# Sliding windows cut from an image batch: from 16-row bands of half the channels to 8-row bands of all channels

## The chip, the cores and the metric

The kernel runs on one core of a Trainium2 chip. The metric is the device time in microseconds (us) of one execution; before the change the median of three runs is 193.44 us (193.0 to 193.72). Profiles are of one execution each. In a profile ACT is ScalarE, DVE is VectorE, POOL is GpSimd and SP is SyncE; DMA engines are the 16 units that move data between the chip's memory (HBM) and the on-chip memory SBUF, which has 128 partitions.

## What is computed

The input `x` has 16 images of 64 channels of 64 by 64 float32 numbers. The output holds every window of 8 by 8 at a stride of 4, so 15 by 15 windows of each image, each with all channels:

```python
result = np.zeros((batch, n_h, n_w, c, window_size, window_size), dtype=np.float32)
for i in range(n_h):
    for j in range(n_w):
        h_start = i * stride
        w_start = j * stride
        result[:, i, j] = x[:, :, h_start:h_start + window_size, w_start:w_start + window_size].copy()
```

Nothing is calculated; numbers are only moved. 16.8 MB go in and 59.0 MB come out, because neighbouring windows overlap. In the output, one window of one image is a contiguous piece of 16 KB: 64 channels times 64 numbers of 4 bytes.

## The kernel before

**Layout.** A partition holds one image, one half of the channels (`ch`, 32 channels) and one of four bands of 16 image rows (`hq`), in the order image, half, band: partition = 8*image + 4*half + band. The tile `L` keeps the whole input in SBUF, 128 KB per partition.

**Loads (lines 49 to 54).** Four chunks of 8 channels, and in each chunk one DMA per band, 16 DMAs of 1 MB. Even bands are issued on SP's queue and odd ones on ACT's. A DMA goes to every fourth partition, and its contiguous rows are 16 image rows of one channel, 4 KB. Four DMAs can be in flight on each of the two queues; a later one waits for an earlier one of its own queue.

**Windows (`window`, lines 97 to 133).** A window position (j, s) says which column j of 15, and which of the four starting rows s inside a band; it makes 128 windows at once, one on each partition. The numbers of all 128 are gathered into a contiguous tile `G`: for s = 0, 1, 2 by one ScalarE copy (line 111). For s = 3, called last, the window runs over the lower edge of the band: VectorE copies the upper half (line 113) and fetches the lower half from the next partition with a stream shuffle (line 114). In the lowest band there is no such window, so a last position has 96 windows and 32 unused partitions.

**Stores (lines 124 to 133).** One indirect DMA of GpSimd (a scatter) writes the 128 rows of `G` to output rows whose numbers stand in a small index tile: `idx`, or `idx_last`, in which the unused partitions have a number that is out of bounds, so that their rows are dropped. A row is half a window, 8 KB. The tiles' framework tracks the scatters by eight semaphores in turn, so a scatter waits for the one eight places earlier. Different stores are declared independent of each other (`free`, line 88).

**Order.** There are 60 window positions, j outside and s inside. The first 12 (`EARLY`, line 135) are made twice, for the first and the second half of the partition's channels: the first halves need only the first two load chunks, so stores can begin when half of the input is there. Such half scatters have 4 KB rows and index tiles of their own (`idx_h`, `idx_hlast`). Second halves and whole windows then alternate (lines 140 to 145). `G` is a ring of nine buffers of 8 KB per partition, counted in 18 half units (line 93); a window is gathered once the scatter that used its buffer has landed. The last two positions (`TAIL`, line 85) go out by seven plain DMAs of SP (line 118), and take buffers that come free a little earlier (`BACK`, line 148).

The functions that the change touches, with the profile's line numbers:

Of the kernel before, what the change touches and what calls it, by code (L numbers as in the profile page):

```python
# [1 line left out]

# [4 lines left out]


@with_exitstack  # L10
def kernel(
    ctx: ExitStack,
    tc: tile.TileContext,
    x: bass.AP,
    window_size: int,
    stride: int,
    out: bass.AP,
):
    nc = tc.nc
    P = nc.NUM_PARTITIONS  # L20

    B, C, H, W = x.shape
    Bo, NH, NW, Co, WSo, WSo2 = out.shape
    WS = int(window_size)
    ST = int(stride)
    assert Bo == B and Co == C and WSo == WS and WSo2 == WS

    f32 = mybir.dt.float32
    i32 = mybir.dt.int32
    ALU = mybir.AluOpType  # L30
    HQ = 4
    CH = P // (B * HQ)
    CL = C // CH
    RB = H // HQ
    NSLOT = RB // ST
    NWIN = NH * NW
    CFREE = CL * WS * WS
    assert HQ == 4 and CH == 2 and WS == 2 * ST

    lpool = ctx.enter_context(tc.tile_pool(name="lpool", bufs=1))  # L40
    ipool = ctx.enter_context(tc.tile_pool(name="ipool", bufs=1))
    gpool = ctx.enter_context(tc.tile_pool(name="gpool", bufs=1))


    L = lpool.tile([P, CL, RB, W], f32)
    x_v = x.rearrange("b (ch cl) (hq r) w -> hq (b ch) cl (r w)", ch=CH, hq=HQ)
    NCH = 4
    cw = CL // NCH
    for k in range(NCH):
        for q in range(HQ):  # L50
            (nc.sync, nc.scalar)[q % 2].dma_start(
                out=L[q::HQ, k * cw : (k + 1) * cw, :, :],
                in_=x_v[q, :, k * cw : (k + 1) * cw, :],
            )


    def itile(name):
        return ipool.tile([P, 1], i32, name=name)

    pi, tb, tq, tc_, idx, idx_last = (itile(n) for n in ("pi", "tb", "tq", "tc", "idx", "idx_last"))  # L60
    nc.gpsimd.iota(pi[:, :], pattern=[[0, 1]], base=0, channel_multiplier=1)  # L61
    nc.vector.tensor_scalar(out=tb[:, :], in0=pi[:, :], scalar1=3, scalar2=None, op0=ALU.logical_shift_right)  # L62
    nc.vector.tensor_scalar(out=tc_[:, :], in0=pi[:, :], scalar1=2, scalar2=1, op0=ALU.logical_shift_right, op1=ALU.bitwise_and)  # L63
    nc.vector.tensor_scalar(out=tq[:, :], in0=pi[:, :], scalar1=HQ - 1, scalar2=None, op0=ALU.bitwise_and)  # L64
    nc.vector.tensor_scalar(out=tb[:, :], in0=tb[:, :], scalar1=float(NWIN * CH), scalar2=None, op0=ALU.mult)  # L65
    nc.vector.tensor_tensor(out=tb[:, :], in0=tb[:, :], in1=tc_[:, :], op=ALU.add)  # L66
    nc.vector.tensor_scalar(out=tc_[:, :], in0=tq[:, :], scalar1=float(NSLOT * NW * CH), scalar2=None, op0=ALU.mult)  # L67
    nc.vector.tensor_tensor(out=idx[:, :], in0=tb[:, :], in1=tc_[:, :], op=ALU.add)  # L68

    nc.vector.tensor_scalar(out=tq[:, :], in0=tq[:, :], scalar1=float(HQ - 1), scalar2=float(2 * B * NWIN * CH), op0=ALU.is_equal, op1=ALU.mult)  # L70
    nc.vector.tensor_tensor(out=idx_last[:, :], in0=idx[:, :], in1=tq[:, :], op=ALU.add)  # L71


    HCL = CL // 2
    idx_h, idx_hlast = itile("idx_h"), itile("idx_hlast")
    for d, e in ((idx_h, idx), (idx_hlast, idx_last)):
        nc.vector.tensor_scalar(out=d[:, :], in0=e[:, :], scalar1=2.0, scalar2=None, op0=ALU.mult)  # L77
    o_v = out.rearrange("b i j (ch cl) r w -> (b i j ch) (cl r w)", ch=CH)
    o_h = out.rearrange("b i j (ch cl) r w -> (b i j ch) (cl r w)", ch=2 * CH)
    nxt = [min(p + 1, 31) for p in range(32)]  # L80

    order = [(j, s) for j in range(NW) for s in range(NSLOT)]


    TAIL, BACK = 2, 3
    o_q = out.rearrange("b i j (ch cl) r w -> i j b ch (cl r w)", ch=CH)

    def free(st):
        tc.declare_no_dep(st.ins, group="stores", reason="each store writes rows of its own")
        tc.add_to_no_dep_group("stores", st.ins)  # L90


    UNITS = 18
    G = [gpool.tile([P, 2 * HCL, WS, WS], f32, name=f"G{n}") for n in range(UNITS // 2)]
    at = 0

    def window(j, s, half):
        nonlocal at
        cols = slice(j * ST, j * ST + WS)
        last = s == NSLOT - 1  # L100
        if half is None:
            n, c0 = 2, 0
            at += at % 2
        else:
            n, c0 = 1, half * HCL
        u = at % UNITS
        at += n
        cs = slice(c0, c0 + n * HCL)
        g = G[u // 2][:, u % 2 * HCL : (u % 2 + n) * HCL, :, :]
        if not last:  # L110
            nc.scalar.copy(out=g, in_=L[:, cs, s * ST : s * ST + WS, cols])  # L111
        else:
            nc.vector.tensor_copy(out=g[:, :, 0:ST, :], in_=L[:, cs, s * ST : RB, cols])  # L113
            nc.vector.stream_shuffle(out=g[:, :, ST:WS, :], in_=L[:, cs, 0:ST, cols], mask=nxt)  # L114
        if (j, s) in order[-TAIL:]:
            g_q = g.rearrange("(m q) c r w -> q m (c r w)", q=HQ)
            for q in range(HQ - 1 if last else HQ):
                free(nc.sync.dma_start(out=o_q[q * NSLOT + s, j], in_=g_q[q]))
            return
        if half is None:  # L120
            o, ix = o_v, (idx_last if last else idx)
        else:
            o, ix = o_h, (idx_hlast if last else idx_h)
        st = nc.gpsimd.indirect_dma_start(  # L124
            out=o,
            out_offset=bass.IndirectOffsetOnAxis(ap=ix[:, 0:1], axis=0),
            in_=g.rearrange("p c r w -> p (c r w)"),
            in_offset=None,
            element_offset=(s * NW + j) * CH * CFREE + (half or 0) * HCL * WS * WS,
            bounds_check=B * NWIN * CH * (1 if half is None else 2) - 1,  # L130
            oob_is_err=False,
        )
        free(st)

    EARLY = 12
    for j, s in order[:EARLY]:
        window(j, s, 0)
    late = list(order[:EARLY])
    rest = list(order[EARLY:])
    while late:  # L140
        for w in late[:2]:
            window(*w, 1)
        for w in rest[:2]:
            window(*w, None)
        late, rest = late[2:], rest[2:]
    for w in rest[:-TAIL]:
        window(*w, None)
    at -= 2 * BACK
    for w in rest[-TAIL:]:
        window(*w, None)  # L150


# [1 line left out]
_INS = ['x', 'window_size', 'stride']  # L154
_OUTS = [((16, 15, 15, 64, 8, 8), 'float32')]

_NUMBERS = {'window_size': 8, 'stride': 4}


# [26 lines left out]
```

## Time and profile before

| What | Value |
|---|---|
| Median of three runs | 193.44 us |
| The profiled execution's own time | 193.19 us |
| Its span, first to last instruction | 191.4 us |
| ACT busy | 86.2 us (45%) |
| POOL busy | 68.0 us (36%) |
| DVE busy | 30.4 us (16%) |
| HBM read and written | 16.78 and 62.65 MB, 415 GB/s over the span |
| DMA packets | 14772, 75.80 MB |

How to read it. The page gives each engine's busy time, and then cuts the span into 40 equal slices of 4.8 us: a digit is the busy share in tenths, and for the DMA engines a second line gives GB/s. Next come the DMA queues: q1 and q10 hold the DMAs of SP and ACT, q0 the scatters of GpSimd; for each the packets, the megabytes, and the time that its packets took as a share of 16 engines' span. A packet here is one row of a transfer, or one of the 4-byte packets that report a DMA's end on an engine, or the 4-byte stand-in of a dropped row. Then follow the chain of work that ended last, the costliest groups of instructions by line, and the DMA issues with the median time from issue to landing. Other views list who waited for whom, the instructions in order of time, and the same figures for a chosen window of time.

Two durations by form that are used below: the ScalarE copy of 128x2048 takes 1896 ns and that of 128x1024 takes 1040 ns; the stream shuffle of 128x1024 takes 1280 ns and that of 128x512 takes 712 ns. A scatter instruction occupies GpSimd for 963 ns.

### The profile page before, as it was taken

What the parts mean: (1) busy time and instruction counts of PE and PEld (TensorE: products, weight loads), DVE (VectorE), ACT (ScalarE), POOL (GpSimd) and SP (SyncE); (2) the same over time, 40 slices, a digit from 0 to 9 for tenths busy, and PEclk for the clock granted to TensorE, in tenths of its full rate; (3) what the DMA queues carried; (4) which work ended last, traced back from release to release, by engine and by line L of the source; (5) the groups of instructions that cost most, each with busy time, mean ns of one, the idle gap of its engine ahead of it and who ended that gap; (6) DMA issues with size and microseconds to landing.
All of it is one profiled execution on the core that took longest, in us unless ns stands there. A gap on an engine that the chain in (4) does not pass through costs nothing.

```text
span 191.4 us, 479 instructions
## 1 busy us (share of the span) xinstructions
DVE 30.4 (16%) x65; ACT 86.2 (45%) x55; POOL 68.0 (36%) x75
## 2 busy tenths in 40 slices
DVE  2000050000232302301221031203030303000030
ACT  0000059400699876364566556565647473300300
POOL 0000028723367666464464343434444444400000
DMA  5999999999999999999999999999999999999785
GB/s 180 419 413 410 410 409 413 416 423 420 417 423 429 423 418 425 407 406 414 410 413 404 414 416 413 404 409 409 411 407 409 411 409 406 416 411 416 325 265 187
DMA packets 14772, 75.80 MB, mean 396 GB/s; under 512 B 2032, under 2 KB 2032, under 8 KB 9008
## 3 DMA queue, kind: packets, MB, share of 16 engines
q0 software_dynamic: 10080, 57.15, 73.3%
q1 hardware_dynamic: 2512, 10.22, 13.8%
q10 hardware_dynamic: 2176, 8.39, 11.1%
q14 instruction: 4, 0.03, 0.0%
HBM read 16.78 MB, written 62.65 MB: 415 GB/s over the span
## 4 chain that ended last, share of the span: by engine, by line
DMA 73%; issue 19%; ACT 2%; POOL 1%; DVE 1%; POOLq 0%; DVEq 0%; PEldq 0%; ACTq 0%
DMA out_dram<-G,idx 60%; DMA out_dram<-G,idx_h 13%; ACT G L111 2%; POOL out_dram L124 1%; DVE G L114 1%; DVE G L113 0%; POOLq L124 0%; POOL pi L61 0%; DVEq L113 0%; PEldq L181 0%; ACTq L111 0%
## 5 line engine op out<-in xcount | busy, mean ns | idle before, releaser
L111 ACT COPY G<-L 128x2048 f32<-128x2048 f32 (+1 forms) x54 | 84.9, 1611 | 69.1 <-DMA out_dram<-G,idx_last 25.1
L124 POOL DMA_INDIRECT out_dram<-G,idx x35 | 33.8, 966 | 45.9 <-DMA out_dram<-G,idx 41.7
L113 DVE COPY G<-L 128x1024 f32<-128x1024 f32 (+1 forms) x18 | 11.1, 614 | 152.1 <-DMA out_dram<-G,idx 76.5
L124 POOL DMA_INDIRECT out_dram<-G,idx_h x18 | 17.4, 964 | 13.9 <-DMA out_dram<-G,idx_hlast 4.8
L114 DVE STREAM_SHUFFLE G<-L 128x1024 f32<-128x1024 f32 (+1 forms) x18 | 19.6, 1091 | 0.0
L124 POOL DMA_INDIRECT out_dram<-G,idx_hlast x6 | 5.9, 989 | 27.8 <-DVE G L114 26.3
L124 POOL DMA_INDIRECT out_dram<-G,idx_last x11 | 10.6, 964 | 10.6 <-DVE G L114 5.8
L111 ACT ACT_TABLE_LOAD x1 | 1.3, 1283 | 25.9 <-DMA L<-in_x_dram 25.9
L62 DVE TENSOR_SCALAR tb<-pi 128x1 int32<-128x1 int32 x1 | 0.2, 154 | 1.0 <-POOL pi L61 1.0
L61 POOL IOTA pi<- 128x1 int32 x1 | 0.1, 119 | 0.4 <-PEq L181 0.4
L114 DVE LOAD_MASK_SELECT G<-L x18 | 0.2, 12 | 0.0
L167 POOL MEMSET const-float32-0.0<- 128x1 f32 x1 | 0.1, 98 | 0.2 <-issue 0.2
L66 DVE CUSTOM_DVE_ANT_0 tb<-tb,tc 128x2 uint16<-128x2 uint16 x1 | 0.2, 160 | 0.0
L68 DVE CUSTOM_DVE_ANT_0 idx<-tb,tc 128x2 uint16<-128x2 uint16 x1 | 0.2, 158 | 0.0
L67 DVE TENSOR_SCALAR tc<-tq 128x1 int32<-128x1 int32 x1 | 0.2, 153 | 0.0
L77 DVE TENSOR_SCALAR idx_hlast<-idx_last 128x1 int32<-128x1 int32 x1 | 0.2, 153 | 0.0
L77 DVE TENSOR_SCALAR idx_h<-idx 128x1 int32<-128x1 int32 x1 | 0.2, 154 | 0.0
L71 DVE CUSTOM_DVE_ANT_0 idx_last<-idx,tq 128x2 uint16<-128x2 uint16 x1 | 0.2, 153 | 0.0
L65 DVE TENSOR_SCALAR tb<-tb 128x1 int32<-128x1 int32 x1 | 0.2, 151 | 0.0
L70 DVE TENSOR_SCALAR tq<-tq 128x1 int32<-128x1 int32 x1 | 0.1, 147 | 0.0
L64 DVE TENSOR_SCALAR tq<-pi 128x1 int32<-128x1 int32 x1 | 0.1, 144 | 0.0
L63 DVE TENSOR_SCALAR tc<-pi 128x1 int32<-128x1 int32 x1 | 0.1, 143 | 0.0
(3 smaller groups left out, 0.3 us busy)
## 6 DMA issues: line engine op xcount, KB each, us to landing
L<-in_x_dram SPq DMA_DIRECT2D x8, 1024.0 KB, 21.1
L<-in_x_dram ACTq DMA_DIRECT2D x8, 1024.0 KB, 19.8
out_dram<-G SPq DMA_DIRECT2D x7, 256.0 KB, 4.2
out_dram<-G,idx POOLq DMA_INDIRECT x35, 18.4
out_dram<-G,idx_h POOLq DMA_INDIRECT x18, 14.1
out_dram<-G,idx_last POOLq DMA_INDIRECT x11, 18.4
out_dram<-G,idx_hlast POOLq DMA_INDIRECT x6, 11.9
```

The source lines that it names most:

```text
L61: nc.gpsimd.iota(pi[:, :], pattern=[[0, 1]], base=0, channel_multiplier=1)
L62: nc.vector.tensor_scalar(out=tb[:, :], in0=pi[:, :], scalar1=3, scalar2=None, op0=ALU.logical_shift_right)
L65: nc.vector.tensor_scalar(out=tb[:, :], in0=tb[:, :], scalar1=float(NWIN * CH), scalar2=None, op0=ALU.mult)
L66: nc.vector.tensor_tensor(out=tb[:, :], in0=tb[:, :], in1=tc_[:, :], op=ALU.add)
L67: nc.vector.tensor_scalar(out=tc_[:, :], in0=tq[:, :], scalar1=float(NSLOT * NW * CH), scalar2=None, op0=ALU.mult)
L68: nc.vector.tensor_tensor(out=idx[:, :], in0=tb[:, :], in1=tc_[:, :], op=ALU.add)
L71: nc.vector.tensor_tensor(out=idx_last[:, :], in0=idx[:, :], in1=tq[:, :], op=ALU.add)
L77: nc.vector.tensor_scalar(out=d[:, :], in0=e[:, :], scalar1=2.0, scalar2=None, op0=ALU.mult)
L111: nc.scalar.copy(out=g, in_=L[:, cs, s * ST : s * ST + WS, cols])
L113: nc.vector.tensor_copy(out=g[:, :, 0:ST, :], in_=L[:, cs, s * ST : RB, cols])
L114: nc.vector.stream_shuffle(out=g[:, :, ST:WS, :], in_=L[:, cs, 0:ST, cols], mask=nxt)
L124: st = nc.gpsimd.indirect_dma_start(out=o, out_offset=bass.IndirectOffsetOnAxis(ap=ix[:, 0:1], axis=0), in_=g.rearrange("p c r w -> p (c r ...
```

## The change

A partition now holds one image and one of eight bands of 8 image rows, with all 64 channels: partition = 8*image + band. `L` still has 128 KB per partition.

- **Loads:** four chunks of 16 channels and eight bands, 32 DMAs of 512 KB, each to every eighth partition (16 of them), in rows of 2 KB. Even bands on SP's queue, odd ones on ACT's.
- **Windows:** a band has two starting rows, so there are 30 window positions; every second one is last, with 112 windows and 16 unused partitions (band 7). The upper half of a last window is now copied by ScalarE too.
- **Stores:** all by scatter, with rows of 16 KB, a whole window; the first six positions are made in two halves of 32 channels with rows of 8 KB. The seven plain stores at the end are gone, as are `TAIL` and `BACK`.
- **Buffers:** `G` is a ring of four buffers of 16 KB per partition (eight half units).
- **Order:** after the early halves, two second halves and one whole window alternate.

```diff
-    HQ = 4
-    CH = P // (B * HQ)
-    CL = C // CH
-    RB = H // HQ
+    NB = P // B
+    RB = H // NB
...
-    L = lpool.tile([P, CL, RB, W], f32)
-    x_v = x.rearrange("b (ch cl) (hq r) w -> hq (b ch) cl (r w)", ch=CH, hq=HQ)
+    L = lpool.tile([P, C, RB, W], f32)
+    x_v = x.rearrange("b c (n r) w -> n b c (r w)", n=NB)
     NCH = 4
-    cw = CL // NCH
+    cw = C // NCH
     for k in range(NCH):
-        for q in range(HQ):
-            (nc.sync, nc.scalar)[q % 2].dma_start(
-                out=L[q::HQ, k * cw : (k + 1) * cw, :, :],
-                in_=x_v[q, :, k * cw : (k + 1) * cw, :],
+        for n in range(NB):
+            (nc.sync, nc.scalar)[n % 2].dma_start(
+                out=L[n::NB, k * cw : (k + 1) * cw, :, :],
+                in_=x_v[n, :, k * cw : (k + 1) * cw, :],
             )
...
-    UNITS = 18
-    G = [gpool.tile([P, 2 * HCL, WS, WS], f32, name=f"G{n}") for n in range(UNITS // 2)]
+    UNITS = 8
+    G = [gpool.tile([P, 2 * HC, WS, WS], f32, name=f"G{n}") for n in range(UNITS // 2)]
...
         if not last:
             nc.scalar.copy(out=g, in_=L[:, cs, s * ST : s * ST + WS, cols])
         else:
-            nc.vector.tensor_copy(out=g[:, :, 0:ST, :], in_=L[:, cs, s * ST : RB, cols])
+            nc.scalar.copy(out=g[:, :, 0:ST, :], in_=L[:, cs, s * ST : RB, cols])
             nc.vector.stream_shuffle(out=g[:, :, ST:WS, :], in_=L[:, cs, 0:ST, cols], mask=nxt)
-        if (j, s) in order[-TAIL:]:
-            g_q = g.rearrange("(m q) c r w -> q m (c r w)", q=HQ)
-            for q in range(HQ - 1 if last else HQ):
-                free(nc.sync.dma_start(out=o_q[q * NSLOT + s, j], in_=g_q[q]))
-            return
...
-    EARLY = 12
+    EARLY = 6
...
-        for w in rest[:2]:
+        for w in rest[:1]:
             window(*w, None)
-        late, rest = late[2:], rest[2:]
-    for w in rest[:-TAIL]:
-        window(*w, None)
-    at -= 2 * BACK
-    for w in rest[-TAIL:]:
+        late, rest = late[2:], rest[1:]
+    for w in rest:
         window(*w, None)
```

More of the change, by code (lines that the diff above doesn't have):

```diff
@@ L30 @@
     ALU = mybir.AluOpType
-    HQ = 4
-    CH = P // (B * HQ)
-    CL = C // CH
-    RB = H // HQ
+    NB = P // B
+    RB = H // NB
     NSLOT = RB // ST
     NWIN = NH * NW
-    CFREE = CL * WS * WS
-    assert HQ == 4 and CH == 2 and WS == 2 * ST
+    CFREE = C * WS * WS
+    assert NB == 8 and WS == 2 * ST and RB == WS
     lpool = ctx.enter_context(tc.tile_pool(name="lpool", bufs=1))
@@ L58, in itile @@
         return ipool.tile([P, 1], i32, name=name)
-    pi, tb, tq, tc_, idx, idx_last = (itile(n) for n in ("pi", "tb", "tq", "tc", "idx", "idx_last"))
+    pi, tb, tn, idx, idx_last = (itile(n) for n in ("pi", "tb", "tn", "idx", "idx_last"))
     nc.gpsimd.iota(pi[:, :], pattern=[[0, 1]], base=0, channel_multiplier=1)
     nc.vector.tensor_scalar(out=tb[:, :], in0=pi[:, :], scalar1=3, scalar2=None, op0=ALU.logical_shift_right)
[L63 to L74, printed above, removed]
+    nc.vector.tensor_scalar(out=tn[:, :], in0=pi[:, :], scalar1=NB - 1, scalar2=None, op0=ALU.bitwise_and)
+    nc.vector.tensor_scalar(out=tb[:, :], in0=tb[:, :], scalar1=float(NWIN), scalar2=None, op0=ALU.mult)
+    nc.vector.tensor_scalar(out=idx[:, :], in0=tn[:, :], scalar1=float(NSLOT * NW), scalar2=None, op0=ALU.mult)
+    nc.vector.tensor_tensor(out=idx[:, :], in0=idx[:, :], in1=tb[:, :], op=ALU.add)
+    nc.vector.tensor_scalar(out=tn[:, :], in0=tn[:, :], scalar1=float(NB - 1), scalar2=float(2 * B * NWIN), op0=ALU.is_equal, op1=ALU.mult)
+    nc.vector.tensor_tensor(out=idx_last[:, :], in0=idx[:, :], in1=tn[:, :], op=ALU.add)
+    HC = C // 2
     idx_h, idx_hlast = itile("idx_h"), itile("idx_hlast")
@@ L77 @@
         nc.vector.tensor_scalar(out=d[:, :], in0=e[:, :], scalar1=2.0, scalar2=None, op0=ALU.mult)
-    o_v = out.rearrange("b i j (ch cl) r w -> (b i j ch) (cl r w)", ch=CH)
-    o_h = out.rearrange("b i j (ch cl) r w -> (b i j ch) (cl r w)", ch=2 * CH)
+    o_v = out.rearrange("b i j c r w -> (b i j) (c r w)")
+    o_h = out.rearrange("b i j (ch cl) r w -> (b i j ch) (cl r w)", ch=2)
     nxt = [min(p + 1, 31) for p in range(32)]
     order = [(j, s) for j in range(NW) for s in range(NSLOT)]
[L85 to L90, printed above, removed]
-    UNITS = 18
-    G = [gpool.tile([P, 2 * HCL, WS, WS], f32, name=f"G{n}") for n in range(UNITS // 2)]
+    UNITS = 8
+    G = [gpool.tile([P, 2 * HC, WS, WS], f32, name=f"G{n}") for n in range(UNITS // 2)]
     at = 0
@@ L104, in window @@
         else:
-            n, c0 = 1, half * HCL
+            n, c0 = 1, half * HC
         u = at % UNITS
         at += n
-        cs = slice(c0, c0 + n * HCL)
-        g = G[u // 2][:, u % 2 * HCL : (u % 2 + n) * HCL, :, :]
+        cs = slice(c0, c0 + n * HC)
+        g = G[u // 2][:, u % 2 * HC : (u % 2 + n) * HC, :, :]
         if not last:
@@ L128, in window @@
             in_offset=None,
-            element_offset=(s * NW + j) * CH * CFREE + (half or 0) * HCL * WS * WS,
-            bounds_check=B * NWIN * CH * (1 if half is None else 2) - 1,
+            element_offset=(s * NW + j) * CFREE + (half or 0) * HC * WS * WS,
+            bounds_check=B * NWIN * (1 if half is None else 2) - 1,
             oob_is_err=False,
         )
-        free(st)
-    EARLY = 12
+        tc.declare_no_dep(st.ins, group="stores", reason="each store writes rows of its own")
+        tc.add_to_no_dep_group("stores", st.ins)
+    EARLY = 6
     for j, s in order[:EARLY]:
```

## The prediction

> **What bounds the kernel now.** I read the page's slices first, then the DMA queues, the waits of the steady part, two windows of the DMA view, and the end. The slices:
>
> ```profile
> DMA  5999999999999999999999999999999999999785
> GB/s 180 419 413 410 410 409 413 416 423 420 417 423 429 423 418 425 407 406 414 410 413 404 414 416 413 404 409 409 411 407 409 411 409 406 416 411 416 325 265 187
> ...
> q0 software_dynamic: 10080, 57.15, 73.3%
> q1 hardware_dynamic: 2512, 10.22, 13.8%
> q10 hardware_dynamic: 2176, 8.39, 11.1%
> ```
>
> From the second slice to the 37th the 16 DMA engines are full at about 411 GB/s. No compute engine is the limit: ScalarE, the busiest, is at 45% of the span. So the kernel is 75.8 MB through full DMA engines, plus a start of about 3 us and an end in which the rate falls (325, 265, 187). A change can act in four ways only: bytes per engine, rate of a row, holes in the stream, the two ends.
>
> The waits on GpSimd say how deep the stream is kept:
>
> ```profile
> POOL out_dram L124 <- DMA out_dram<-G,idx: 43.5, 29, 2.2
> ...
> out_dram<-G,idx POOLq DMA_INDIRECT x35, 18.4
> ```
>
> A scatter waits for the scatter eight places earlier, and takes 18.4 us from issue to landing: eight times 1 MB lie in the queues. GpSimd waits, but the DMA engines don't.
>
> The DMA view of 33 to 44 us, when loads (q1, q10) and early stores (q0) run together:
>
> ```profile
> q10 hardware_dynamic: 439, 1.73, 38.3%
> q1 hardware_dynamic: 439, 1.67, 36.9%
> q0 software_dynamic: 441, 1.22, 27.6%
> ```
>
> Packets per queue are equal: 439, 439, 441. Each engine takes one row from each queue in turn, whatever its bytes (q0 has fewer because its turns include small completion packets and the dropped rows of last windows). The rows are 4 KB on all three queues here. Followed one by one, the packet records show the same on each engine: row of q10, row of q1, row of q0.
>
> The end, in the windows view (columns: window and length, the engines' busy time, clock, DMA share, GB/s):
>
> ```profile
> 180.00:191.40 11.40, 1.89 (x3) 1.11 (x1) 0.00 (x0) 1.00 0.66 224
> ```
>
> 224 GB/s for 11.4 us are 2.55 MB; at 411 GB/s they need 6.2 us, so 5.2 us are lost there, while the last two windows are copied and go out in seven stores of SyncE.
>
> [...]
>
> **The change, part by part**, against the profiled span of 191.4 us (its execution took 193.19 us, so 1.8 us lie around it; the median of the runs, 193.44, is 0.25 above).
>
> *Copies.* 128x2048 takes 1896 ns and 128x1024 1040 ns on ScalarE, so 128x4096 about 3.6 us. A pair of windows (one full copy, one half copy now on ScalarE too) needs 3.6+1.9 = 5.5 us, its stores 4.2 MB or less, near 10 us. The shuffle (712 ns at 512, 1280 at 1024 elements) comes to about 2.4 us at 2048, beside it on VectorE. Hidden. The index work shrinks at 2 us, under the loads: nothing.
>
> *Depth.* Four buffers of 2 MB. When a scatter lands, its buffer's next window needs copy 3.6, GpSimd 1.0 (963 ns) and 3.2 us to the first packet (in before the first scatter instruction ends at 28.4, the first store packet starts at 31.6): 7.8 us. Three windows of 5.1 us are queued meanwhile, 15.3 us: covered, with 7 us to spare. Fewer buffers would pay; these don't. In the steady part nothing is lost.
>
> *Rows.* A 4 KB row takes 159 ns and an 8 KB row 314 (medians of the packet records): about 4 ns each plus the bytes. Loads become 2 KB rows, 512 per engine at 81.5 = 41.7 us against 256 at 159 = 40.7: +1.0[...]. Stores become 225 rows of 16 KB per engine instead of 450: -0.9. Together +0.1.
>
> *A hole after the loads: +6.9.* The first copies still wait for half of the loads (25.9 us). The first scatter then needs a 1.9 us copy, not a short shuffle, so the first store packet comes near 33.4. By then 8.4+(33.4-25.2)*0.411 = 11.8 MB are loaded, 5.0 MB remain. The early stores are 3*(128+112)*8 KB = 5.9 MB. Per turn an engine now moves 8 KB of stores (less completion packets and dropped rows, 6.8 KB) against two rows of 2 KB (3.9 KB): stores get 64%, 263 GB/s, loads 148. The stores are gone in 22.4 us, at 55.8, when 1.7 MB of loads are left: 4.1 us more, to 59.9. Every next window needs all loads: landing 0.7 (before: last load packet 48.9, copy 49.6), copy 1.9+0.1, GpSimd 1.0, first packet 3.2: 6.9 us with idle DMA engines. Today equal rows gave stores a third, and their backlog covered this. Bounds 0 and 8.
>
> *Uneven engines: +9.4.* A last window drops partitions with band 7. [...] half of the engines hold bands 4 to 7 and lose two rows of eight in 15 of 30 windows, the others none. Those carry 30*8 = 240 rows of 16 KB, against a mean of 225: 30 rows of 8 KB more than today's 450, at 314 ns. Bounds 0 (eight consecutive partitions per engine) and 9.4.
>
> *Ports: +8.* A load of band n reaches partitions n, n+8, n+16 and so on[...]. Both queues go through the bands in the same order. [...] the 8.4 MB before the first copies take 41 instead of 20.4 us (+20), and what is left after the early stores another +10: +30. If the queues are one DMA apart of four, half of that, +15. Lower bound 0, as the trace shows no port limit. [...] How far an engine's buffers hide it I can't see; I take 8.
>
> *End: -4.* The last windows go through the scatter queue, which holds three windows when the last copy starts. Of the 5.2 us I give back 4. Bounds -5 and 0, where engines end unevenly.
>
> Sum: 191.4+0.1+6.9+9.4+8-4 = 211.8, and with 1.8 around it 213.6; with the median's place 213.7.
>
> **Rivals.** *Forecast* (0.50): uneven engines, hole and a port limit; own range 205.6 to 236 from the port bounds.
> *No port limit* (0.20): 203.8+1.8 = 205.6. For it: no load row in the trace was slowed. [...]
> *Even engines, hole only* (0.20): 191.4+0.1+6.9-4+1.8 = 196.2. For it: nothing shows how a scatter's rows are dealt.
> *Faster* (0.10): even engines and no hole, because queues take turns by bytes: 191.4+0.1-4+1.8 = 189.3. It decides from the point where 6.9 us of early stores (2.8 MB) are left when the loads end: 3.1 MB of stores beside 5.0 of loads, a share of 38% or less; equal bytes would give 33%. Against: 439, 439 and 441 packets.
>
> **How the numbers follow.** About 0.5% is what a measurement tells from no change here. Faster is the last case but for its edge, 0.09; a hole half as deep with even engines is within 0.5%, 0.06; the rest, 0.85, is slower. The range leaves out the fast case and the full port limit: 195 to 230.
>
> **What would show it.** Hole: a slice or two of zero DMA near 60 us or later, and the store queue empty before it. Ports: slices well under 400 GB/s and the first copy later than 26 us. Uneven engines: alternate windows at a lower DMA share late in the span, around 365 GB/s. End: over 300 GB/s until the last 3 us. Wrong: first copy at 26 us and full slices to the end.

## The result, and the profile after

| | Before | After |
|---|---|---|
| Median | 193.55 us (193.0 to 193.72) | 224.44 us (222.19 to 230.76) |
| Profiled execution, and its span | 193.19, 191.4 us | 226.41, 224.6 us |
| First copy on ScalarE or VectorE | 25.9 us | 43.2 us |
| Last load lands | 49.6 us | 83.4 us |

The changed kernel is slower. Its executions differ among themselves by up to 9 us, for a reason that stays open, so the ratio of 1.1487 (95% interval 1.1455 to 1.152) and the comparisons below go by its shorter ones (222.19 and 222.46, +28.6 over before), while the page below is of a longer one.

The same lines of the page that were shown of before, now of the kernel after (slices of 5.6 us, then the queues):

```profile
DMA  6999999999999999999999999999999999999942
GB/s 135 204 230 218 222 236 208 235 220 223 236 209 242 419 425 430 436 417 439 420 436 426 432 425 429 387 426 400 432 388 388 422 391 423 385 426 391 382 213 90
...
q0 software_dynamic: 5184, 58.99, 62.1%
q1 hardware_dynamic: 4352, 8.39, 17.3%
q10 hardware_dynamic: 4352, 8.39, 17.3%
```

The two lines must be read together. The digits say that the DMA engines are full from the second slice on; the rates say that for the first 13 slices they move about 220 GB/s, where before moved 411. The bytes of q10 are the same 8.39 MB in both pages, but its packets now hold 17.3% of a longer span instead of 11.1%: 38.9 us of 16 engines instead of 21.2. The loads are what became slow. No slice is empty, so the hole that I forecast isn't there. At the end the rate falls to 213 and 90.

Stretches of the kernel after in the windows view (columns: window and length, busy time of VectorE, ScalarE and GpSimd with instructions, clock, DMA share, GB/s):

```profile
3.00:62.00 59.00, 3.65 (x6) 0.00 (x0) 0.00 (x0) 1.00 1.07 223
62.00:72.00 10.00, 0.00 (x0) 9.61 (x7) 4.67 (x5) 1.00 1.07 224
72.00:84.00 12.00, 0.55 (x2) 0.61 (x2) 1.26 (x2) 1.00 1.03 410
84.00:140.00 56.00, 15.57 (x15) 35.07 (x17) 15.41 (x16) 1.00 1.01 428
140.00:205.00 65.00, 16.87 (x14) 38.50 (x14) 12.52 (x13) 1.00 0.96 405
...
212.00:222.00 10.00, 0.00 (x0) 0.00 (x0) 0.00 (x0) 1.00 0.49 210
```

Until 72 us loads run alone, at 223 or 224 GB/s. From the moment stores join them the rate is whole again, and for 56 us it is 428 GB/s, above the 411 of before. Then it falls to 405 at a share of 0.96. A finer cut of that stretch shows that the fall comes every second time, at the pace of two windows in 10 us:

```profile
156.00:161.00 5.00, 0.76 (x1) 2.02 (x2) 0.96 (x1) 1.00 1.01 429
161.00:166.00 5.00, 2.03 (x2) 3.57 (x2) 0.96 (x1) 1.00 0.91 387
166.00:171.00 5.00, 0.44 (x1) 2.16 (x1) 0.96 (x1) 1.00 0.99 419
```

At the end a share of 0.49 and 210 GB/s say that half of the engines have nothing left.

ScalarE's start, in the timeline of the kernel after (start, length, engine, line, operation):

```profile
0.73 61.48 ACTq L49 DMA_DIRECT2D L<-in_x_dram  x16
...
43.20 1.28 DVE L102 STREAM_SHUFFLE G<-L 128x1024 f32<-128x1024 f32 x1
...
62.38 1.28 ACT L99 ACT_TABLE_LOAD   x1 [62.38 <-DMA L<-in_x_dram]
63.67 1.90 ACT L99 COPY G<-L 128x2048 f32<-128x2048 f32 x1
```

Half of the loads are in at 43.2 us, when VectorE begins. ScalarE begins 19 us later, because its own instruction queue still holds loads: it issues 16 of them, four may be in flight, and so the last is issued only when the 12th has landed: it landed at 61.6 us, and the issue ended at 62.2. Copies stand behind that in the same queue. In the waits of the kernel after (total, times, longest) this is one line:

```profile
POOL out_dram L107 <- ACT G L99: 132.8, 18, 64.9
...
ACT L99 <- DMA L<-in_x_dram: 62.4, 1, 62.4
```

GpSimd waits for ScalarE, and ScalarE for a load; the first store packet moves near 72 us. Before, ScalarE issued eight loads, the last at 22 us, ahead of the 25.9 us at which it could copy anyway.

### The profile page after: what moved, and what is told of

It reads as the page before. It is cut to its first block, busy times and chain, and to the rows that moved or that the text cites. A ratio compares the mean times of both kernels' runs of the same rounds, so it can differ in the third digit from the quotient of the medians.

```text
span 224.6 us, 332 instructions
## 1 busy us (share of the span) xinstructions
DVE 38.0 (17%) x45; ACT 83.8 (37%) x37; POOL 35.2 (16%) x41
## 3 DMA queue, kind: packets, MB, share of 16 engines
q1 hardware_dynamic: 4352, 8.39, 17.3%
q10 hardware_dynamic: 4352, 8.39, 17.3%
## 4 chain that ended last, share of the span: by engine, by line
DMA 50%; issue 37%; POOL 2%; DVE 1%; ACT 1%; POOLq 1%; DVEq 0%; PEldq 0%; ACTq 0%
DMA out_dram<-G,idx_last 36%; DMA out_dram<-G,idx_hlast 14%; POOL out_dram L107 2%; DVE G L102 1%; ACT G L101 1%; POOLq L162 1%; POOLq L107 0%; DVE idx L64 0%; DVE tb L60 0%; DVE idx_h L73 0%; DVEq L102 0%; DVE tb L62 0%; POOL pi L59 0%; DVE idx L63 0%; DVE tn L66 0%
## 5 line engine op out<-in xcount | busy, mean ns | idle before, releaser
L99 ACT COPY G<-L 128x4096 f32<-128x4096 f32 (+1 forms) x18 | 54.5, 3034 | 45.1 <-DMA out_dram<-G,idx 30.7
L102 DVE STREAM_SHUFFLE G<-L 128x2048 f32<-128x2048 f32 (+1 forms) x18 | 36.8, 2056 | 0.2
L101 ACT COPY G<-L 128x2048 f32<-128x2048 f32 (+1 forms) x18 | 28.9, 1612 | 13.6 <-DMA out_dram<-G,idx_last 11.0
L107 POOL DMA_INDIRECT out_dram<-G,idx x12 | 11.6, 963 | 53.3 <-ACT G L99 53.3
L107 POOL DMA_INDIRECT out_dram<-G,idx_h x6 | 5.9, 989 | 79.4 <-ACT G L99 79.4
L107 POOL DMA_INDIRECT out_dram<-G,idx_last x12 | 11.6, 963 | 36.5 <-issue 36.0
```

The lines of the kernel that those rows point to most:

```text
L101: nc.scalar.copy(out=g[:, :, 0:ST, :], in_=L[:, cs, s * ST : RB, cols])
L107: st = nc.gpsimd.indirect_dma_start(out=o, out_offset=bass.IndirectOffsetOnAxis(ap=ix[:, 0:1], axis=0), in_=g.rearrange("p c r w -> p (c r ...
```

## The experiments

**The changed kernel again**, beside three of the kernels below (queues by band half, split loads, drops spread) on one chip.

> The changed kernel once more, for the comparison with the runs beside it and for another profile. All theories: 222 to 223 us.

Measured: 226.97 us (222.08 to 228.32), the same picture.

**Loads: queues by band half.** The changed kernel with bands 0 to 3 on SP's queue and 4 to 7 on ScalarE's. In the changed kernel the loads of a queue land one after another (ScalarE's first at 8.7 us, its 12th at 61.6, 4.8 us each), in turn with those of the other queue. So bands 0 and 1 travel together, then 2 and 3, 4 and 5, 6 and 7: for most of the time two of the same half. With the edit the two are of different halves. What the recorded texts call ports stands for whatever bands of one half have in common; no trace shows what that is.

```diff
-            (nc.sync, nc.scalar)[n % 2].dma_start(
+            (nc.sync, nc.scalar)[n // 4].dma_start(
```

> Changed kernel, but bands 0 to 3 are loaded from SP's queue and bands 4 to 7 from ACT's[...]. Rows, DMAs and bytes are the same. Port theory: the loads run near 400 GB/s instead of 216, the first ScalarE copy comes near 35 us instead of 62, and the time falls to 197 us (195 to 201). Rival, that 2 KB rows or DMAs of 16 partitions are slow in themselves: no change, 222.

Measured: 202.6 us (201.85 to 203.6), ratio to before 1.0503 (1.0466 to 1.0541). The load phase in its windows:

```profile
3.00:10.00 7.00, 0.00 (x0) 0.00 (x0) 0.00 (x0) 1.00 1.07 240
10.00:48.00 38.00, 3.65 (x6) 6.18 (x5) 2.07 (x2) 1.00 1.06 369
```

Rows, bytes and instructions are those of the changed kernel; only which bands travel together differs, and 19.5 us come back (222.08 to 202.6). So this time went to two bands of the same half travelling together, and not to the 2 KB rows. It ended 5.6 us above what I expected, because the first 7 us still run at 240 GB/s and the rest at 369, not 411. In the packet records (start and duration of every packet, which the DMA view sums up) a 2 KB row takes a median of 160 ns in the changed kernel, about 93 here, and 84 once only stores run beside it.

**Before, with split loads.** The kernel before, each load split into two DMAs of 16 partitions, eight apart, in the changed kernel's order; rows stay 4 KB. Where a DMA of before reaches every fourth partition, two that travel together now lie in the same half of each eight partitions (places 0 to 3, or 4 to 7).

```diff
-    x_v = x.rearrange("b (ch cl) (hq r) w -> hq (b ch) cl (r w)", ch=CH, hq=HQ)
+    x_v = x.rearrange("b (ch cl) (hq r) w -> ch hq b cl (r w)", ch=CH, hq=HQ)
...
-        for q in range(HQ):
-            (nc.sync, nc.scalar)[q % 2].dma_start(
-                out=L[q::HQ, k * cw : (k + 1) * cw, :, :],
-                in_=x_v[q, :, k * cw : (k + 1) * cw, :],
+        for n in range(8):
+            (nc.sync, nc.scalar)[n % 2].dma_start(
+                out=L[n::8, k * cw : (k + 1) * cw, :, :],
+                in_=x_v[n // HQ, n % HQ, :, k * cw : (k + 1) * cw, :],
```

> Kernel before, with only its loads changed: each is split into two DMAs of 16 partitions, every eighth partition, in the order and on the queues of the changed kernel, with rows of 4 KB as before. Port theory: loads at 210 to 230 GB/s, ScalarE's first copy near 60 us, the time near 222 us (218 to 226). Rival, short rows: 193 to 196.

Measured: 223.16 us (222.02 to 223.3), ratio 1.1535 (1.1494 to 1.1576). Its load phase, and then the same stretch of the kernel before:

```profile
3.00:30.00 27.00, 0.00 (x0) 0.00 (x0) 0.00 (x0) 1.00 1.03 219
```

```profile
3.00:26.00 23.00, 0.08 (x1) 0.11 (x1) 0.00 (x0) 1.00 1.02 411
```

219 against 411 GB/s at a DMA share of 1.0 in both. A 4 KB row takes 309 ns instead of 159. This edit alone, in the old layout with its old rows and stores, costs 29.8 us. It makes 16 loads on ScalarE's queue too, and the first copy is held to 63.7 us as in the changed kernel; so the 29.8 us hold both the halved rate and the hold, which were not tried apart.

**Drops spread over the engines.** The changed kernel with other row numbers for last windows: in every second group of four images band 3 is dropped and band 7 writes to its place. (In those images band 3's last windows hold band 7's numbers.) Followed one by one in the packet records of the changed kernel, half of the engines carry three rows of a last scatter, a dropped one, three rows and a dropped one; the other half carry eight rows and drop none.

```diff
...
+    nc.vector.tensor_scalar(out=t3[:, :], in0=tm[:, :], scalar1=3.0, scalar2=big, op0=ALU.is_equal, op1=ALU.mult)
+    nc.vector.tensor_scalar(out=t7[:, :], in0=tm[:, :], scalar1=7.0, scalar2=-(big + 4 * NSLOT * NW), op0=ALU.is_equal, op1=ALU.mult)
...
+    nc.vector.tensor_tensor(out=idx_last[:, :], in0=idx_last[:, :], in1=t3[:, :], op=ALU.add)
```

> Changed kernel, but which rows a last window drops is spread: in the second and fourth quarter of the partitions band 3 is dropped and band 7 goes to band 3's output row, so that each engine drops one of its eight rows if rows are dealt in groups of four partitions. The bytes and the rows written are the same in number; some output rows hold another window's numbers. Theory of uneven engines: the fullest engines go from 240 to 225 rows of 616 ns, 9 us less, 213 us (211 to 216), and the half-rate end of 12 us is gone. Rival, that rows are dealt evenly already and the end is slow for another reason: 222.

Measured: 219.65 us (213.17 to 222.86). The shortest execution of each, 213.17 against 222.08, differ by -8.9. Two stretches of its end, then one that starts earlier:

```profile
204.00:212.00 8.00, 0.00 (x0) 0.00 (x0) 0.00 (x0) 1.00 1.00 426
212.00:218.00 6.00, 0.00 (x0) 0.00 (x0) 0.00 (x0) 1.00 0.36 153
```

```profile
136.00:204.00 68.00, 16.98 (x14) 38.52 (x14) 14.26 (x15) 1.00 1.01 424
```

Full until 212, where the changed kernel ran 10 us on half of its engines; and 424 GB/s on the way there, where the changed kernel fell to 405. The same edit on top of the queues by band half gives a sharper size:

> Changed kernel with the queues by half and the spread drops together (the rows dropped in last windows are one of each engine's eight; some output rows hold another window's numbers). Theory of uneven engines: 9.2 us less than the queues by half alone, 193.4 us (192 to 196), and over 400 GB/s until the last 3 us. Rival, that the uneven end is hidden behind something else: 200 to 203.

Measured: 195.53 us (194.75 to 196.3), ratio 1.0107 (1.0074 to 1.014), 7.1 us below the queues by band half alone. Its end:

```profile
180.00:190.00 10.00, 0.00 (x0) 0.00 (x0) 0.00 (x0) 1.00 1.00 426
190.00:194.50 4.50, 0.00 (x0) 0.00 (x0) 0.00 (x0) 1.00 0.15 62
```

**Balanced with a real output.** The queues by band half, and the same aim as before without changed numbers: in odd columns a last window is put together in the lower band (its upper half fetched from the partition before), so that band 0 is unused there and band 7 in even columns.

```diff
...
+        elif j % 2:
+            nc.scalar.copy(out=g[:, :, ST:WS, :], in_=L[:, cs, 0:ST, cols])
+            nc.vector.stream_shuffle(out=g[:, :, 0:ST, :], in_=L[:, cs, s * ST : RB, cols], mask=prv)
...
-            o, ix = o_v, (idx_last if last else idx)
+            o, ix = o_v, ((idx_up if j % 2 else idx_last) if last else idx)
```

> Changed kernel with the queues by half, and every window where it belongs: last windows of even columns are put together in the upper partition (band 7 unused), those of odd columns in the lower one (the upper half by shuffle from the partition before, band 0 unused). The engines then carry 226 and 224 rows of 16 KB, not 240 and 210. Theory of uneven engines: as with the spread drops, 195.5 us (194 to 197). Rival, that spread drops gained for another reason: 202.

Measured: 195.88 us (195.37 to 197.8), ratio 1.0158 (1.0114 to 1.0202); 6.7 us below the queues by band half alone. The uneven engines are priced at 7 us, by two edits. Its load phase, which is used further down:

```profile
3.00:10.00 7.00, 0.00 (x0) 0.00 (x0) 0.00 (x0) 1.00 1.07 240
10.00:43.00 33.00, 3.67 (x6) 0.69 (x1) 0.00 (x0) 1.00 1.06 362
43.00:56.00 13.00, 1.16 (x2) 10.14 (x8) 5.92 (x6) 1.00 1.05 386
```

**Before, without its end by plain stores.** The last two windows go out by scatter and in the order of the ring, everything else as before.

```diff
-        if (j, s) in order[-TAIL:]:
-            g_q = g.rearrange("(m q) c r w -> q m (c r w)", q=HQ)
-            for q in range(HQ - 1 if last else HQ):
-                free(nc.sync.dma_start(out=o_q[q * NSLOT + s, j], in_=g_q[q]))
-            return
...
-    at -= 2 * BACK
```

> Kernel before with one part alone: the last two windows go out by scatter like all others, in ring order, and the seven stores of SP are gone. The prediction's term for the end: 4 us less, 189.4 us. Rival, that the engines end so unevenly that nothing is won: 193 to 194.

Measured: 194.31 us against 193.23, ratio 1.0057 (1.0039 to 1.0075): 1.1 us slower, not 4 faster. Stretches of its end, and then of the end of before:

```profile
180.00:182.00 2.00, 0.00 (x0) 0.00 (x0) 0.00 (x0) 1.00 1.02 426
...
186.00:188.40 2.40, 0.00 (x0) 0.00 (x0) 0.00 (x0) 1.00 0.43 178
188.40:192.40 4.00, 0.00 (x0) 0.00 (x0) 0.00 (x0) 1.00 0.00 0
```

```profile
180.00:182.00 2.00, 0.27 (x1) 1.11 (x1) 0.00 (x0) 1.00 0.48 201
...
190.00:191.40 1.40, 0.00 (x0) 0.00 (x0) 0.00 (x0) 1.00 0.00 0
```

The wait for the last copies is gone: 426 GB/s in 180 to 182 us instead of 201, and in the packet records the last row ends at 188.3 us instead of 190.1. But then 4.1 us pass in which nothing moves, and with the plain stores only 1.3. That is 1.8 us won and 2.8 lost. What fills the 4.1 us isn't shown.

**Where the higher store rate comes from: ScalarE instead of VectorE for upper halves.** After 84 us the changed kernel moves 428 GB/s, before 411. One suspect was the VectorE copy that the change moved.

```diff
-            nc.vector.tensor_copy(out=g[:, :, 0:ST, :], in_=L[:, cs, s * ST : RB, cols])
+            nc.scalar.copy(out=g[:, :, 0:ST, :], in_=L[:, cs, s * ST : RB, cols])
```

> Kernel before with one part alone: the upper half of a last window is copied by ScalarE and not by VectorE, as in the changed kernel. The stores of the changed kernel run at 425 to 430 GB/s, those of before at 409. Theory that VectorE's copy hinders the writing of scatters: the rate after 100 us rises to 420 or more and the time falls to 189 us. Rival, that the longer rows are what is faster: 193 to 194.

Measured: 193.43 us against 193.23, ratio 1.0008 (0.9997 to 1.002), and 411 GB/s in 100 to 140 us. That theory fell.

**Row length alone.** The balanced kernel, with each whole window stored by two scatters of 8 KB rows instead of one of 16 KB rows.

```diff
...
+        for m in (0, 1) if half is None else (half,):
+            gm = g if half is not None else g[:, m * HC : (m + 1) * HC, :, :]
...
+                element_offset=(s * NW + j) * CFREE + m * HC * WS * WS,
```

> The balanced kernel of four load chunks, with every whole window stored by two scatters with rows of 8 KB, one for each half of the channels, instead of one with rows of 16 KB. Theory that the longer row makes the stores of the changed kernel faster (428 GB/s against 409 before): the rate after 100 us falls to about 410 and the time rises by 5 to 6 us over the balanced kernel (201 us). Rival, that the row's length does nothing and the layout or the number of scatters in flight is the reason: within 1 us of the balanced kernel.

Measured: 201.21 us (200.58 to 202.1), 5.3 us above the balanced kernel. Three stretches of the balanced kernel, then of the one with half rows:

```profile
56.00:100.00 44.00, 11.47 (x13) 28.69 (x14) 12.52 (x13) 1.00 1.01 430
100.00:140.00 40.00, 10.92 (x9) 22.55 (x9) 8.66 (x9) 1.00 1.01 427
140.00:180.00 40.00, 9.80 (x8) 22.01 (x8) 7.70 (x8) 1.00 1.01 424
```

```profile
56.00:100.00 44.00, 11.32 (x12) 28.50 (x13) 18.31 (x19) 1.00 1.01 426
100.00:140.00 40.00, 10.81 (x10) 23.03 (x9) 16.39 (x17) 1.00 1.01 415
140.00:180.00 40.00, 10.61 (x9) 22.89 (x9) 15.42 (x16) 1.00 1.01 409
```

Copies and bytes are equal; only GpSimd's instructions and the rows differ. Up to 100 us, while both still store some half windows, the rates are nearly equal; after that the rate falls by 3 to 4%, to what the kernel before has. Longer rows (or fewer and larger scatters, which this doesn't separate) give 5.3 us. The loss lies in the rows and not in pauses between them, for the DMA share is 1.01 in both: by the packet records of these two stretches an 8 KB row takes 318 and 323 ns on average, a 16 KB row 617 and 620.

**The hole.** Three kernels ask whether it is real. First the queues by band half with two chunks of 1 MB loads instead of four of 512 KB, so that copies begin early.

```diff
-    NCH = 4
+    NCH = 2
```

> Changed kernel with the queues by half (bands 0 to 3 on SP, 4 to 7 on ACT) and two load chunks instead of four, so 16 load DMAs of 1 MB: ScalarE has issued its last load once the first half has landed, and its copies start then, not at three quarters. The comparison is the kernel with the queues by half alone (202.6 us). Theory of the hole: the first copy comes near 29 us, the early stores are gone near 58, the loads end near 64, and 6.9 us with idle DMA engines follow: 208 us (206 to 211). Rival, that there is no hole because the stores and loads end together: 202.

Measured: 207.31 us, ratio 1.0755 (1.0714 to 1.0797), 4.7 above the queues by band half.

```profile
62.00:67.00 5.00, 2.51 (x6) 2.57 (x2) 0.40 (x1) 1.00 0.11 21
67.00:72.00 5.00, 2.30 (x1) 5.00 (x3) 2.47 (x3) 1.00 0.80 328
```

Five microseconds at 21 GB/s, while ScalarE and VectorE make the first windows that need all loads: the forecast hole. In the packet records no row moves from 63.5 to 68.1 us. Next, the balanced kernel with two chunks and eight early positions instead of six.

```diff
-    NCH = 4
+    NCH = 2
...
-    EARLY = 6
+    EARLY = 8
```

> The balanced kernel with two load chunks of 1 MB DMAs, so that the copies start at half of the loads, and eight early half windows instead of six (7.9 MB), so that their backlog covers the end of the loads. If loads that run beside stores are no longer slowed and no hole is left: first stores near 37 us with 12.3 MB loaded, the other 63.5 MB at 426 GB/s, 149 us, so 188 and 1.8: 190 us (188 to 193), faster than before. Rival, that a hole stays because the early stores still end first: 194 to 197.

Measured: 200.1 us (199.0 to 201.21), ratio 1.0357 (1.0324 to 1.0391). A clear miss.

```profile
60.00:66.00 6.00, 0.00 (x0) 0.00 (x0) 0.00 (x0) 1.00 1.03 428
66.00:70.00 4.00, 2.81 (x6) 2.87 (x3) 0.70 (x1) 1.00 0.03 9
70.00:80.00 10.00, 3.34 (x3) 10.00 (x6) 5.08 (x6) 1.00 0.94 383
```

Two more positions bring the early stores from 5.9 to 7.9 MB, and they still ended with the loads, at 66 us; the stream moved 420 GB/s in 40 to 60 us. After that the rate is 383 GB/s in 70 to 80 us at a share of 0.94. ScalarE is busy in all of these 10 us, so the copies that fill the empty store queue again probably hold it; that is not shown apart. Last, twelve early positions, 11.8 MB:

```diff
-    EARLY = 8
+    EARLY = 12
```

> The balanced kernel with two load chunks and twelve early half windows (11.8 MB) instead of eight. At a share of 64% against 36%, and 4.5 MB of loads left when the stores begin, the early stores must be more than 9.9 MB to outlast the loads by the 7 us that the next windows need. Theory of the hole: with 11.8 MB no slice is empty, and the time is 4.7 us less than with eight, 195.4 us or less (191 to 196). Rival, that the late start of the next windows comes from the buffers and not from the loads: a hole stays, 199 to 201.

Measured: 192.52 us (191.86 to 194.71) against 193.15 on the same chip, ratio 0.9983 (0.9954 to 1.0012). The slices of this kernel:

```profile
DMA  5999999999999999999999999999999999999990
GB/s 126 326 374 382 374 378 378 377 424 417 418 428 421 426 421 433 430 423 452 406 433 423 445 418 433 416 437 423 430 420 426 416 430 437 416 426 413 433 385 31
```

The hole is gone. What is left under the rate of before is the loads' opening, 326 GB/s in the second slice and then 374 to 382. The time is about 30 us below the changed kernel's, and can't be told from the kernel before.

## Why the prediction was right in its direction, and short in its size

Slower, inside the range; the likeliest time was 213.7 us, 10.7 below the median and 8.6 below the shorter executions. The steps in turn:

- **Ports: the mis-sized term.** Its upper bound of 30 us is half the rate while loads run alone. The prediction put what is left of that as "How far an engine's buffers hide it I can't see; I take 8", an estimate between 0 and 30 that no row of the profile gave. Next to nothing is hidden: a row takes a median of 160 ns instead of 84 for as long as loads run alone. Queues by band half give back 19.5 us of this. Another 7.6 us stay lost even then: the balanced kernel, which loads in the same way, moves 240 GB/s in 3 to 10 us, 362 in 10 to 43 and 386 in 43 to 56, 18.65 MB, which at 411 take 45.4 of its 53 us. About 2.3 us of these are the shorter rows (an engine's 512 rows at 84 ns, instead of 256 at 159). That the rest has the same cause is my estimate and not shown, for no run loads 2 KB rows in DMAs to every fourth partition. Together that is about 25 us where I took 8. That loads slow one another was forecast rightly, and which of them do was shown by two runs (160 ns for a row instead of about 93, 309 instead of 159); through what they do is not shown. That the upper bound of 30 comes so near is in part luck: it had stores beside the loads from 33 us on, and they came at 72, by the next point.
- **"The first copies still wait for half of the loads"** failed. I counted the loads that a copy needs, and not those that stand ahead of it in ScalarE's queue: 16 loads with four in flight hold it until three quarters have landed. All 16 loads that ScalarE issued counted there, and its first copy came at 63.7 us instead of the 27.2 of before. What the hold costs by itself was not tried; in the changed kernel it keeps the loads alone for longer, and so acts together with their low rate.
- **The hole: +6.9 forecast, 0 in the changed kernel.** Because of that hold: stores came so late (72 us) that they outlasted the loads (83.4 us). The mechanism is real, for once copies begin early the hole stands in the windows (21 GB/s for 5 us), and a backlog of 7.9 MB still leaves one while 11.8 MB doesn't. Its size was too large: it lasts 4.6 us with six early positions and 4.4 with eight. The prediction took 3.2 us from the end of a scatter instruction to its first packet, as at the first scatter of before; after the hole it is 0.6 us.
- **Uneven engines: +9.4 forecast, 6.7 and 7.1 measured** (8.9 between lowest executions). That half of the engines lose two rows of eight is what the packet records show: half of the engines carry eight full rows in every scatter, and they end at 221.4 to 221.9 us; the others carry six in each last one, and end at 212.3 to 212.8. The forecast dips in alternate windows are there, but only from about 140 us on, and at 387 GB/s rather than 365: by the rate (405 against 428 for 65 us) they cost some 3.5 us. The rest comes at the end, 10 us at 210 GB/s. Up to then several scatters are queued, and a lighter engine probably goes on to the next one.
- **Rows of the stores: -0.9 forecast, -5.3 measured.** I took a 16 KB row as two 8 KB rows less 4 ns, from the medians of 4 KB and 8 KB rows. The median of 16 KB is already 17 ns less (611 against 314), and the averages, on which the rate depends, lie 19 to 27 ns apart in 100 to 180 us (318 to 323 for 8 KB with half rows and before, 617 to 620 for 16 KB in the balanced kernel). Over 225 rows per engine that is 4.3 to 6.0 us. The length is not all of it: the changed kernel's own 8 KB rows, which in 100 to 140 us go out among 16 KB rows, take 310 on average.
- **End: -4 forecast.** It did not come: the same edit on before costs 1.1 us. The term counted what a wait for copies takes from the stream, and left out the time after the last row. That grows from 1.3 to 4.1 us there, and is 2.7 us in the changed kernel (221.9 to 224.6).

The sum of measured terms: 19.5 + 7.6 + 6.7 - 5.3 = 28.5 us, with the end at about nothing; measured are 28.6. That they agree so closely is no proof: the 7.6 are worked out from rates, the terms come from different kernels, and the end is left out. The total of the prediction was nearer than its terms, and that is luck: the terms of ports and end together were some 21 us too low, hole, uneven engines and rows some 13 us too high.

DMAs of 16 partitions, two at a time in the same half of each eight, gave 219 to 224 GB/s, against 411 for DMAs to every fourth partition. The rival *No port limit* is excluded by the two experiments on loads; *Even engines* by the spread drops; *Faster* by both.

Still open: what the hold costs by itself, why rows of 8 KB take longer on average among their like than among rows of 16 KB, what holds the loads at 362 to 386 GB/s with two halves at a time, and what passes between the last row and the end.

## What to carry to other kernels

Before re-tiling a load, write down which partitions each DMA in flight reaches, and whether those that run at the same time lie in the same half of each eight: a stride of eight partitions with both queues in the same half came with 219 GB/s here instead of 411 (split loads), with every byte and row as it was, and with 223 in the changed kernel. Where only the degree of a mechanism is unknown, work out the size that it has when nothing softens it, and don't settle on a value in between for which no row of the profile speaks: here the full size was the nearer one. And for a copy that shares an engine with DMA issues, look at the queue ahead of it as well as at its data.

## What the runs showed of the hardware

- **A DMA share of 1.0 is not full rate.** In 20 to 40 us of the changed kernel each load queue holds 53% of 16 engines while both together move 224 GB/s; a row that takes 160 ns instead of 84 counts as busy for all of them. The DMA view there:

```profile
q10 hardware_dynamic: 1160, 2.24, 53.5%
q1 hardware_dynamic: 1162, 2.24, 53.1%
```

- **Two loads at a time in the same half of each eight partitions take almost double the time for a row, at both lengths tried:** 309 ns instead of 159 at 4 KB, 160 instead of 84 at 2 KB. With stores of 8 KB rows among them the stream of the changed kernel is whole again (410 GB/s in 72 to 84 us); with three early stores of 4 KB rows, in the kernel before with split loads, it is so in part (308 GB/s in 52 to 62 us).
- **Two queues on different halves recover most of the rate:** 369 GB/s with 512 KB loads and 374 to 382 with 1 MB, against 411 in before. Part of what is missing is the row: one of 2 KB in 84 ns comes to 390 GB/s on 16 engines.
- **After 100 us, streams of 16 KB rows run at 424 to 428 GB/s, streams of 8 KB rows at 409 to 415.**
- **A queue's share goes by its rows:** followed one by one in the packet records, engines take one row from each queue in turn, with 8 KB stores beside 2 KB loads as with 4 KB on all queues (before). In 74 to 80 us of the changed kernel q0 has 250 packets with 1.68 MB, and q10 has 255 with 0.49 MB.
